# The gated convolution's three input projections as block products in seven multiplications

## The chip, the cores and the metric

One core of one Trainium2 chip runs the whole program in a single launch. The metric is the device time of that launch in microseconds (us), the median of several executions; 2549.22 us before the change (three runs, 2545.19 to 2549.35). A profile is one further execution.

## The reference

Two residual layers over 1024 tokens of width 1024, in fp32. Each layer is a mixer, a cross-attention into 256 memory tokens and a squared-ReLU MLP, each behind an RMS norm. The mixer of layer 0 is differential attention beside causal pooling; that of layer 1 is the one that is changed here:

```python
def odd_mixer(h, w_in, conv_w, w_out):
    S = h.shape[1]
    proj = h @ w_in
    b_gate = proj[..., :CONV_DIM]
    c_gate = proj[..., CONV_DIM:2 * CONV_DIM]
    z = c_gate * proj[..., 2 * CONV_DIM:]
    zp = jnp.pad(z, ((0, 0), (CONV_WIDTH - 1, 0), (0, 0)))
    y = zp[:, 0:S] * conv_w[0]
    for tap in range(1, CONV_WIDTH):
        y = y + zp[:, tap:tap + S] * conv_w[tap]
    return (b_gate * y) @ w_out
```

`h` is the normed residual stream, `w_in` is 1024 x 3072 and `w_out` 1024 x 1024.

## The kernel before

The residual stream is kept transposed: eight tiles of 128 channels by 1024 tokens. TensorE multiplies in a reduced fp32 format, so every operand is cut into a high and a low half: ScalarE copies the high half (line 72 of the profile), VectorE subtracts it from the source (line 73), and a product is the sum of three multiplications, high by high, high by low and low by high. The names `wh` and `wl` are the two halves of a weight tile; `wr` is the tile as it came from DRAM.

Two kinds of product stand in the program. `gemm` computes one tile of 128 output channels: eight tiles of input channels, three multiplications, two halves of 512 tokens, so 48 matmuls of 128 x 512, two PSUM banks. `split_gemm` computes two output tiles at once by a block scheme (2 x 2 blocks: halves of the tokens against the two tiles) in seven multiplications instead of eight: seven steps of 12 matmuls, 84 for two tiles instead of 96. For it the weights' pair is combined into four groups (`w_cut`, lines 149 to 153: four half-size VectorE operations, then a cut for each group), the input channels come as four combinations of pairs of tiles (class `Split`: `combine`, lines 259 to 262, and a cut for each), and every step's bank is added to the two output tiles by an `evac` function, since one step serves several results. Steps 0, 2, 4 and 6 write on in the same bank, so the next of them waits until the one before was read.

The MLPs (`mlp`: `m0a`, `m0b` in layer 0, `m1a`, `m1b` in layer 1) and the query projections (`c0q`, `c1q`) use `split_gemm`. The convolution (`conv_mixer`, names `cv0c` to `cv7b`) uses `gemm`: for each of eight channel tiles the products c, x and b, then on VectorE the gate, the scaling by the norm, two taps and the multiplication with b, and a cut into `Y`, the operand of the output product `cvo` (`residual`).

The convolution's operand is made at the end of the MLP before it. `m0b` runs over four chunks of the hidden width and four pairs of output tiles; in the last chunk each finished pair is scaled by the norm's weight and cut, in the product that follows. The scaling by the norm's 1 / rms comes later: squares are summed over the tiles (`m0b_acc`), TensorE transposes the sums (`m0b_n`, line 332), VectorE reduces them (333, 335), POOL takes the power (336), TensorE spreads the result (`m0b_b`, 345) and ScalarE writes it out (`m0b_rbc`).

Weights are loaded on SP's queue in the order of the list `order`, at most four tiles ahead (`WR`), each as soon as the tile whose buffer it takes has been cut; `wh` and `wl` have two buffers each, so a cut waits until TensorE is through with the group before last. Activations live in 44 equal slots. Results go to DRAM on ScalarE's queue and come back on SP's. Each engine works through its queue in order; a scheduler sets these orders by the order of the code and by priorities.

Of the kernel before, what the change touches and what calls it, by code (L numbers as in the profile page):

```python
# [40 lines left out]
def hybrid_trunk(ctx: ExitStack, tc: tile.TileContext, xT, memT, vecs, lams, rel, onehot, negrow, invcnt,  # L41
# [40 lines left out]
    order = [(FLAT, w_in[8])]  # L82
# [35 lines left out]
    def w_cut():  # L118
        u, g = state["unit"], state["group"]
        if u >= len(order):  # L120
            return
        shape = list(order[u][0])
# [7 lines left out]
        else:  # L130
            a, b = raw[0], raw[1]
            if g == 0 and u in tails:
                t = sb.tile(shape, F32, tag="wt", bufs=1, name=f"wt{u}")
# [694 lines left out]
    def residual(act, g_col, name, split=False):  # L828
# [3 lines left out]
        r = [None, None]  # L832
        for n in range(KT):
# [22 lines left out]
            else:  # L856
                ps = gemm(act, f"{name}_{n}")
# [160 lines left out]
    def mlp(l, X, nrm, g_next, name):  # L1018
# [76 lines left out]
        nx, nn = Act(), Norm(f"{name}b")  # L1095
        fin = g_next is None
        for c in range(4):
            for p in range(KT // 2):
                t, ahead = ahead, []
                tail = fin and c == 3 and p == KT // 2 - 1  # L1100
# [13 lines left out]
                todo = [rest, {1: [look]}]  # L1114
# [14 lines left out]
                def done(i, t=t, p=p):  # L1129
                    def run():  # L1130
                        n = 2 * p + i
                        if fin:
                            hd[n] = t[i]
                        else:
                            operand(nx, n, t[i], g_next, f"{name}b")
                        nn.add(t[i])
                    return run
# [140 lines left out]
```

## Time and profile before

| | us |
|---|---|
| median of three runs | 2549.22 |
| the profiled execution | 2544.53 |
| its span | 2542.8 |
| projections of the convolution, 1332.74 to 1595.67 of the span | 262.93 |
| one of their 24 products | 10.88 |
| output product `cvo` | 81.60 |

In the profile's rows PE is TensorE's matmul and PEld its weight load, DVE is VectorE, ACT ScalarE, POOL GpSimd, SP the queue that loads; L with a number is a line of the kernel. Matmul ends are modelled and matmuls overlap, so the time of many is read from the chain of waits or from a stretch, not from one duration. Idle time in a row is that of the engine just before, with what ended it.

### The profile page before, as it was taken

The page shows a single profiled execution, that of the slowest core. Times are in us where ns is not written, and L with a number is a line of the kernel's source. Part 1 is how long each engine was busy: PE and PEld are TensorE (multiplying, and loading weights), DVE is VectorE, ACT ScalarE, POOL GpSimd, SP SyncE. Part 2 cuts the span into 40 slices and gives each one's busy share as a digit, 9 for nine tenths or more (in the row PEclk, how much of TensorE's full clock was granted, in tenths as well). Part 3 has the DMA queues.
Part 4 walks back from the last instruction along what each step waited for, and adds up shares of the span by engine and source line. Part 5 has one row for each costly group of instructions (what it writes and reads, how often), then busy time and mean ns, then how long its engine had stood idle before and what let it go on. Part 6 is the DMA issues. An engine that isn't in the chain of part 4 may idle for free.

```text
span 2542.8 us, 29713 instructions
## 1 busy us (share of the span) xinstructions
PE 2498.8 (98%) x11522; PEld 2048.1 (81%) x11522; DVE 1763.8 (69%) x2339; ACT 1073.4 (42%) x1513; POOL 25.7 (1%) x24
## 2 busy tenths in 40 slices
PE   9999999999999999999999999999999999999997
PEld 6777778888878888788888888888887888778886
DVE  7777764766677777888784433576667777888876
ACT  5455664445443334443341111344544333434432
POOL 0000000000000000000000000000000000000001
PEclk9999999999999999999999999999999999999998
DMA  5111255221424346877641111422133444777752
GB/s 175 34 34 42 75 169 204 100 83 42 141 88 171 139 145 239 293 270 261 243 154 59 50 50 46 145 75 92 58 117 116 159 160 153 269 266 259 281 207 92
DMA packets 108429, 365.88 MB, mean 144 GB/s; under 512 B 12416, under 2 KB 14848, under 8 KB 108288
## 3 DMA queue, kind: packets, MB, share of 16 engines
q1 hardware_dynamic: 74880, 252.82, 29.5%
q10 hardware_dynamic: 33408, 111.16, 11.4%
q8 instruction: 91, 1.49, 0.2%
q14 instruction: 50, 0.41, 0.0%
HBM read 249.91 MB, written 114.03 MB: 143 GB/s over the span
## 4 chain that ended last, share of the span: by engine, by line
PE 89%; DVE 6%; ACT 2%; DMA 2%; issue 1%; POOL 0%; SPq 0%; ACTq 0%; DVEq 0%; POOLq 0%
PE m0a_x L277 7%; PE m1a_x L277 7%; PE m1b_x L277 7%; PE m0b_x L277 6%; PE m1a_yz L277 5%; PE m0a_yz L277 5%; PE m1b_yz L277 5%; PE m0b_yz L277 4%; PE cvo L201 3%; PE X L201 3%; PE c1o L201 3%; PE c0o L201 3%; PE kv_ps L742 3%; PE qkv L201 2%; PE c1q_x L277 2%; PE c0q_x L277 2%
## 5 line engine op out<-in xcount | busy, mean ns | idle before, releaser
L72 ACT ACTIVATE wh<-wr 128x1024 fp32r<-128x1024 f32 (+1 forms) x318 | 305.6, 961 | 777.7 <-PE m1b_yz L277 137.5
L73 DVE TENSOR_TENSOR wl<-wr,wh 128x1024 fp32r<-128x1024 f32 (+1 forms) x318 | 350.3, 1101 | 135.1 <-ACT wh L72 130.3
L72 ACT ACTIVATE wh<-wt 128x1024 fp32r<-128x1024 f32 x72 | 76.0, 1055 | 60.0 <-PE m0b_x L277 16.5
L73 DVE TENSOR_TENSOR wl<-wt,wh 128x1024 fp32r<-128x1024 f32 x72 | 87.8, 1219 | 0.9 <-ACT wh L72 0.9
L201 PE MATMUL X<-Y,wh 128*128 128x512 f32 x256 | 69.8, 389 | 0.0
L581 ACT ACTIVATE s_p<-s,s_negm 128x128 f32<-128x128 f32 (+7 forms) x64 | 47.3, 739 | 33.6 <-DVE s_negm L580 30.3
L201 PEld LDWEIGHTS X<-Y,wh 128*128 128x128 f32 x256 | 48.1, 188 | 10.0
L149 DVE TENSOR_TENSOR wt<-wr 128x512 f32<-128x512 f32 x71 | 48.8, 687 | 6.8 <-DMA wr<-in_w_dram 3.1
L150 DVE TENSOR_TENSOR wt<-wr,wt 128x512 f32<-128x512 f32 x71 | 48.9, 689 | 1.3
L152 DVE TENSOR_TENSOR wr<-wr,wr 128x512 f32<-128x512 f32 x71 | 48.7, 687 | 1.0
L153 DVE TENSOR_TENSOR wr<-wr,wt 128x512 f32<-128x512 f32 x71 | 48.6, 684 | 0.0
L1028 ACT ACTIVATE m0a_r<-m0a_r 128x1024 f32<-128x1024 f32 x32 | 33.9, 1061 | 32.0 <-DVE m0a_r L1027 31.9
L1028 ACT ACTIVATE m1a_r<-m1a_r 128x1024 f32<-128x1024 f32 x32 | 33.9, 1060 | 32.0 <-DVE m1a_r L1027 31.8
L580 DVE TENSOR_REDUCE s_negm<-s 128x1 f32<-128x128 f32 (+7 forms) x64 | 46.6, 750 | 0.2
L1042 DVE TENSOR_TENSOR m0a_r<-m0a_r,m0a_yz 128x512 f32<-128x512 f32 x32 | 21.9, 685 | 31.3 <-PE m0a_yz L277 31.1
L1042 DVE TENSOR_TENSOR m1a_r<-m1a_r,m1a_yz 128x512 f32<-128x512 f32 x32 | 21.9, 685 | 31.3 <-PE m1a_yz L277 31.1
L1038 ACT ACTIVATE m0a_r<-m0a_x 128x512 f32<-128x512 f32 x32 | 19.1, 598 | 55.7 <-PE m0a_x L277 53.8
L1038 ACT ACTIVATE m1a_r<-m1a_x 128x512 f32<-128x512 f32 x32 | 19.1, 598 | 55.5 <-PE m1a_x L277 53.9
L201 PE MATMUL X<-Y,wl 128*128 128x512 f32 x128 | 40.7, 389 | 0.0
L277 PE MATMUL m0b_x<-m0A,wh 128*128 128x512 f32 x128 | 39.5, 390 | 0.7 <-DVE m0b0h L1112 0.7
L277 PE MATMUL m0a_x<-c0o_x,wh 128*128 128x512 f32 x128 | 39.6, 390 | 0.0
L277 PE MATMUL m1a_x<-c1o_x,wh 128*128 128x512 f32 x128 | 39.5, 390 | 0.0
(2681 smaller groups left out, 7678.9 us busy)
## 6 DMA issues: line engine op xcount, KB each, us to landing
wr<-in_w_dram SPq DMA_DIRECT2D x128, 512.0 KB, 4.0
m0f<-m0a_d SPq DMA_DIRECT2D x48, 512.0 KB, 6.4
m1f<-m1a_d SPq DMA_DIRECT2D x48, 512.0 KB, 6.0
wr<-in_wkv_dram SPq DMA_DIRECT2D x32, 512.0 KB, 3.5
m0a_d<-m0a_r ACTq DMA_DIRECT2D x32, 512.0 KB, 2.8
m1a_d<-m1a_r ACTq DMA_DIRECT2D x32, 512.0 KB, 2.9
wr<-in_conv_in_dram SPq DMA_DIRECT2D x24, 512.0 KB, 3.6
wr<-in_wq_dram SPq DMA_DIRECT2D x16, 512.0 KB, 3.6
```

The source lines that it names most:

```text
L72: nc.scalar.activation(hi, src, AF.Copy)
L73: nc.vector.tensor_sub(lo, src, f32(hi))
L149: nc.vector.tensor_add(t[:, 4:], b[:, :4], b[:, 4:])
L150: nc.vector.tensor_sub(t[:, :4], a[:, :4], t[:, 4:])
L152: nc.vector.tensor_sub(a[:, :4], b[:, :4], a[:, :4])
L153: nc.vector.tensor_add(a[:, 4:], a[:, 4:], t[:, :4])
L201: nc.tensor.matmul(ps, wt[:, k, :], act.part(k, i, h), start=(k == 0 and wt is hi and i == 0), stop=(k == ks - 1 and wt is lo))
L277: nc.tensor.matmul(banks[b], w[a][:, 4 * (i % 2) + j, :], act.part(g, s, j, c), start=(new and j == 0 and n == 0), stop=(j == nk - 1 and n ...
L580: nc.vector.tensor_reduce(s["negm"][:, m : m + 1], ps[:, :L], axis=AX.X, op=ALU.max, negate=True)
L581: nc.scalar.activation(s["pr"][m][:, :L], ps[:, :L], AF.Exp, bias=s["negm"][:, m : m + 1], accum_out=s["den"][:, m : m + 1])
L742: nc.tensor.matmul(ps[mt], mem["x"][i][k // 4][:, k % 4, mt * P : (mt + 1) * P], w[j][:, kk, :], start=(k == 0 and n == 0), stop=(k == KT ...
L1028: nc.scalar.activation(t, t, AF.Square)
```

## The change

The three projections become twelve products by `split_gemm`, each for two channel tiles (`cv0c`, `cv0x`, `cv0b` to `cv3b`), 84 matmuls each. Their weights are loaded as pairs, with the input halves in the order that the block scheme wants. Their results are added up in slots of SBUF, from where VectorE makes the gate (now with the square of the norm's scale, `cv_rsq`), the taps and the closing multiplication, hung as hooks on the steps of later products.

The operand is made as a `Split`. For the pairs 0 and 1 of the MLP's last chunk combination 0 is cut at once and combinations 1 to 3 are written to DRAM and read back when they are needed; those of the pairs 2 and 3 stay in slots. The first two products, c and x of the pair 0, run in turns: two steps of the one, two of the other, by combinations 0, 1 and then 2 and 3 (`in_turns`, and the table `seq` that sets the order of the weight cuts); their hooks read, cut and add up squares. The MLP's last product takes the step order `TAIL`, and in its last chunk the inputs for the additions are asked for at step 5 instead of 1. The output product's first two tiles are begun together, six of the eight input tiles first (`late`).

```diff
--- before.py
+++ after.py
...
+            turns.add(len(order))
+            for j in range(KT // 2):
+                order += [(FLAT, conv_in[i * KT + 2 * j], conv_in[i * KT + 2 * j + 1]) for i in (1, 2, 0)]
...
+        tails.add(len(order) - 1)
...
+    seq, u = [], 0
+    while u < len(order):
+        groups = 4 if len(order[u]) > 2 else 1
+        if u in turns:
+            seq += [(u, 0), (u + 1, 0), (u, 1), (u + 1, 1), (u, 2), (u, 3), (u + 1, 2), (u + 1, 3)]
+            u += 2
+        else:
+            seq += [(u, g) for g in range(groups)]
+            u += 1
...
+                t = slot(f"wt{u}", F32, shape) if u - 1 in turns else sb.tile(shape, F32, tag="wt", bufs=1, name=f"wt{u}")
...
+    def in_turns(one, two):
+
+        for it, n in ((one, 2), (two, 2), (one, 2), (two, 2), (one, 4), (two, 4)):
+            for _ in range(n):
+                next(it, None)
...
+        two = []
+        if late:
+            two = [(w_next(), psg(f"{name}_0")), (cuts[state["used"]], psg(f"{name}_1"))]
+            state["used"] += 1
+            for ks in (range(KT - 2), range(KT - 2, KT)):
+                for w, ps in two:
+                    for k in ks:
+                        steps([(h, ps[:, half(h)]) for h in range(2)], w, act, k)
...
+                ps = two.pop(0)[1] if two else gemm(act, f"{name}_{n}")
...
+        nx, nn = Split(f"{name}x"), Norm(f"{name}b")
         fin = g_next is None
+        xd, raws_x, kept = {}, {}, {}
+
+
+        def scale(t, p, h):
+            raws_x[p, 2 * h] = slot(f"{name}x{p}_r{h}")
+            for i in range(2):
+                nc.scalar.activation(raws_x[p, 2 * h][:, i * H : (i + 1) * H], t[i][:, half(h)], AF.Copy,
+                                     scale=col(g_next + 2 * p + i))
+
+        def sums(p):
+            raws_x[p, 1], raws_x[p, 3] = (slot(f"{name}x{p}_t{i}") for i in range(2))
+            raws_x[p, 3] = raws_x[p, 3][:, :H]
+            combine(raws_x[p, 0], raws_x[p, 2], raws_x[p, 1], raws_x[p, 3])
+
+        def first_group(p):
+            nx.group(0, p, raws_x[p, 0])
+
+        def put(p):
+            for g in range(1, 4):
+                xd[p, g] = dp.tile([P, S if g < 3 else H], F32, name=f"{name}x{p}_d{g}")
+                nc.scalar.dma_start(xd[p, g], raws_x.pop((p, g)))
+
+        def get(g):
+            for p in range(2):
+                x = slot(f"{name}xf{g}_{p}")
+                raws_x[p, g] = x if g < 3 else x[:, :H]
+                nc.sync.dma_start(raws_x[p, g], xd[p, g])
+
+        def made(g, *ps):
+            for p in ps:
+                nx.group(g, p, raws_x.pop((p, g)))
...
-                todo = [rest, {1: [look]}]
+                todo = [rest, {5 if c == 3 and not fin else 1: [look]}]
...
+                if tail and not fin:
+                    todo.append({2: [lambda: get(1)], 4: [lambda: made(1, 0)],
+                                 5: [lambda: scale(t, p, 0), lambda: first_group(p), lambda: made(1, 1)],
+                                 6: [lambda: made(1, 2), lambda: get(2)]})
...
+                elif p < 2:
+                    rest = {1: [lambda t=t, p=p: scale(t, p, 0), lambda t=t, p=p: scale(t, p, 1)],
+                            2: [lambda p=p: first_group(p), lambda p=p: sums(p)], 3: [lambda t=t: nn.add(t[0])],
+                            4: [lambda p=p: put(p), lambda t=t: nn.add(t[1]), keep]}
+                elif p == 2:
+                    rest = {2: [lambda t=t, p=p: scale(t, p, 0), lambda t=t, p=p: scale(t, p, 1)],
+                            3: [lambda p=p: first_group(p), lambda p=p: sums(p)], 4: [keep]}
+                    kept[2] = t
+                else:
+                    scale(t, p, 1)
+                    sums(p)
+                    made(1, 3)
+                    nx.late = ({2: [lambda: get(3)], 3: [lambda: made(2, 0)], 4: [lambda: made(2, 3)],
+                                5: [lambda: made(3, 0, 1)], 6: [lambda: made(3, 2, 3)]},
+                               {2: [lambda: made(2, 1)], 3: [lambda: made(2, 2)],
+                                4: [lambda: nn.add(kept[2][0]), lambda: nn.add(kept[2][1]), keep],
+                                5: [lambda t=t: nn.add(t[0])], 6: [lambda t=t: nn.add(t[1]), nn.stage1]})
...
-        hooks = with_norm(nrm)
-        Y = Halves()
-        for j in range(KT):
-            nm = f"{name}{j}"
-            psc = gemm(X, f"{nm}c", hooks.pop(0) if hooks else None)
-            cg, z = slot(f"{nm}_cg"), slot(f"{nm}_z")
-            if nrm.rbc is not None:
-                nc.vector.tensor_mul(cg, psc, nrm.rbc)
-            psx = gemm(X, f"{nm}x", hooks.pop(0) if hooks else None)
+        Y, ys = Halves(), {}
+        sq = {}
+
+        def product(nm, hooks, first=False, run=True):
+            r = [slot(f"{nm}_r{n}") for n in range(2)]
+
+            def evac(n, h, ps, new):
+                d = r[n][:, half(h)]
+                if new:
+                    nc.scalar.activation(d, ps, AF.Copy)
+                else:
+                    nc.vector.tensor_add(d, d, ps)
+
+            steps = split_steps(X, nm, evac, hooks, first=first)
+            if not run:
+                return r, steps
+            for _ in steps:
+                pass
+            return r
+
+        def parts(k):
+            return lambda: Y.put(f"{name}g{k}_", k, ys.pop(k))
+
+        def squared():
+            sq[0] = slot(f"{name}_rsq")
+            nc.scalar.activation(sq[0], nrm.rbc, AF.Square)
+
+        for j in range(KT // 2):
+            nm, last = f"{name}{j}", j == KT // 2 - 1
             if j == 0:
-                nc.vector.tensor_mul(cg, psc, nrm.rbc)
-            nc.vector.tensor_mul(z, psx, nrm.rbc)
-            nc.vector.tensor_mul(z, z, cg)
-            y = slot(f"{nm}_y")
-            nc.scalar.activation(y, z, AF.Copy, scale=col(C_CONV + 16 + j))
-            nc.vector.scalar_tensor_tensor(y[:, 1:], z[:, : S - 1], col(C_CONV + 8 + j), y[:, 1:],
-                                           op0=ALU.mult, op1=ALU.add)
-            nc.vector.scalar_tensor_tensor(y[:, 2:], z[:, : S - 2], col(C_CONV + j), y[:, 2:],
-                                           op0=ALU.mult, op1=ALU.add)
-            nc.vector.tensor_mul(y, y, nrm.rbc)
-            psb_ = gemm(X, f"{nm}b")
-            nc.vector.tensor_mul(y, y, psb_)
-            Y.put(f"{nm}g", j, y)
-        return residual(Y, g_next, f"{name}o", split=True)
+                c, one = product(f"{nm}c", X.late[0], first=True, run=False)
+                x, two = product(f"{nm}x", X.late[1], run=False)
+                in_turns(one, two)
+            else:
+                c = product(f"{nm}c", merged(before, {4: [parts(0)]} if last else {}))
+                x = product(f"{nm}x", {1: [parts(1)], 3: [parts(2)]} if last else {})
+
+            def gate(n, c=c, x=x):
+                def run():
+                    nc.vector.tensor_mul(c[n], c[n], x[n])
+                    nc.vector.tensor_mul(c[n], c[n], sq[0])
+                return run
+
+            def taps(n, z=c, j=j):
+                def run():
+                    k = 2 * j + n
+                    y = ys[k] = slot(f"{name}_y{k}")
+                    nc.scalar.activation(y, z[n], AF.Copy, scale=col(C_CONV + 16 + k))
+                    for d in (1, 2):
+                        nc.vector.scalar_tensor_tensor(y[:, d:], z[n][:, : S - d], col(C_CONV + 8 * (2 - d) + k),
+                                                       y[:, d:], op0=ALU.mult, op1=ALU.add)
+                return run
+
+            def scaled(n, j=j):
+                return lambda: nc.vector.tensor_mul(ys[2 * j + n], ys[2 * j + n], nrm.rbc)
+
+            hooks = {0: [gate(0)], 1: [taps(0)], 2: [gate(1)], 3: [taps(1)], 4: [scaled(0)], 5: [scaled(1)]}
+            if j == 0:
+                hooks = {1: [nrm.stage2, squared], 2: [gate(0)], 3: [taps(0)], 4: [gate(1)], 5: [taps(1)],
+                         6: [scaled(0), scaled(1)]}
+            if last:
+                hooks = merged(hooks, {3: [parts(3)], 5: [parts(4)], 6: [parts(5)]})
+            b = product(f"{nm}b", hooks)
+
+            def times(n, j=j, b=b):
+                return lambda: nc.vector.tensor_mul(ys[2 * j + n], ys[2 * j + n], b[n])
+
+            before = {1: [times(0)], 2: [times(1)]}
+        for n in range(2):
+            times(n)()
+            parts(KT - 2 + n)()
+        return residual(Y, g_next, f"{name}o", split=True, late=True)
...
+    g["conv_in"] = tiles(a["conv_w_in"][0])[..., halves, :]
```

The rows that follow are the engines' instruction streams as built. In the names, `m0b3h6` and `m0b3h7` are the MLP's last two output tiles, `m0x_g_p` with h or l is the half of combination g of pair p, `m0xf` a combination read back from DRAM, `wl98`, `wl99` and `wl100` are the low halves of the convolution's first weights for c, x and b; L1112 became L1170 and L333, L335 became L352, L354.

VectorE at the end of the MLP, before:

```order
L1112 TENSOR_TENSOR m0b3h7_10594<-m0b3h7_10594,m0b3_3_yz_10707 128x512
L73 TENSOR_TENSOR wl97_3_10783<-wr97_1_10512,wh97_3_10782 128x512
L1112 TENSOR_TENSOR m0b3h7_10594<-m0b3h7_10594,m0b3_3_x_10706 128x512
L1112 TENSOR_TENSOR m0b3h6_10592<-m0b3h6_10592,m0b3_3_yz_10707 128x512
L73 TENSOR_TENSOR wl98_0_10821<-wr98_0_10650,wh98_0_10820 128x1024
L76 SCALAR_TENSOR_TENSOR m0b_x6l_10840<-m0b3h6_10592,vec_76,m0b_x6h_10839 128x1024
L1112 TENSOR_TENSOR m0b3h7_10594<-m0b3h7_10594,m0b3_3_x_10706 128x512
L324 TENSOR_TENSOR m0b_acc_10450<-m0b_acc_10450,m0b_sq_10843 128x1024
L76 SCALAR_TENSOR_TENSOR m0b_x7l_10847<-m0b3h7_10594,vec_76,m0b_x7h_10846 128x1024
L324 TENSOR_TENSOR m0b_acc_10450<-m0b_acc_10450,m0b_sq_10850 128x1024
L73 TENSOR_TENSOR wl99_0_10858<-wr99_0_10652,wh99_0_10857 128x1024
```

The same place now:

```order
L1170 TENSOR_TENSOR m0b3h7_10697<-m0b3h7_10697,m0b3_3_x_10734 128x512 x2
L73 TENSOR_TENSOR m0x_0_3l_10850<-m0x3_r0_10846,m0x_0_3h_10849 128x1024
L1170 TENSOR_TENSOR m0b3h7_10697<-m0b3h7_10697,m0b3_3_yz_10735 128x512
L1170 TENSOR_TENSOR m0b3h6_10695<-m0b3h6_10695,m0b3_3_yz_10735 128x512
L73 TENSOR_TENSOR m0x_1_1l_10854<-m0xf1_1_10778,m0x_1_1h_10853 128x1024
L1170 TENSOR_TENSOR m0b3h6_10695<-m0b3h6_10695,m0b3_3_x_10734 128x512
L73 TENSOR_TENSOR wl98_0_10872<-wr98_0_10665,wh98_0_10871 128x1024
L73 TENSOR_TENSOR m0x_1_2l_10881<-m0x2_t0_10797,m0x_1_2h_10880 128x1024
L162 TENSOR_TENSOR wr98_0_10665<-wr98_1_10667,wr98_0_10665 128x512
L163 TENSOR_TENSOR wr98_0_10665<-wr98_0_10665,wt98_10873 128x512
L267 TENSOR_TENSOR m0x3_t0_10904<-m0x3_r1_10901,m0x3_r0_10846 128x512
L73 TENSOR_TENSOR wl99_0_10921<-wr99_0_10820,wh99_0_10920 128x1024
```

The cut of `wl98` stood ahead of the last addition to `m0b3h7`; it now stands behind the last addition to `m0b3h6` and behind the cut of `m0x_1_1l`, whose source comes from DRAM.

TensorE at the start of the convolution now:

```order
L295 MATMUL m0b3_3_x_10734<-m0A3_2_3h_10338,wl97_3_10817 128x512
L295 MATMUL cv0c_x_10918<-m0x_0_0h_10469,wh98_0_10871 128x512
L295 MATMUL cv0c_x_10918<-m0x_0_0l_10470,wh98_0_10871 128x512
L295 MATMUL cv0c_yz_10919<-m0x_0_0h_10469,wh98_0_10871 128x512
L295 MATMUL cv0c_yz_10919<-m0x_0_0l_10470,wh98_0_10871 128x512
L295 MATMUL cv0c_x_10918<-m0x_0_0h_10469,wl98_0_10872 128x512
L295 MATMUL cv0c_x_10918<-m0x_0_1h_10622,wh98_0_10871 128x512
```

Four matmuls with `wh98` stand ahead of the first that needs `wl98`; before, the first product's matmuls had the same high and low weights in turn.

VectorE where the norm's sums are reduced, before:

```order
L324 TENSOR_TENSOR m0b_acc_10450<-m0b_acc_10450,m0b_sq_10850 128x1024
L73 TENSOR_TENSOR wl99_0_10858<-wr99_0_10652,wh99_0_10857 128x1024
L333 TENSOR_REDUCE m0b_ms_8465<-m0b_n0_10894 128x4
L333 TENSOR_REDUCE m0b_ms_8465<-m0b_n1_10900 128x4
L335 TENSOR_SCALAR m0b_ms_8465<-m0b_ms_8465 128x8
L73 TENSOR_TENSOR wl100_0_10929<-wr100_0_10786,wh100_0_10928 128x1024
```

And now, at the end of the x product:

```order
L343 TENSOR_TENSOR m0b_acc_10492<-m0b_acc_10492,m0b_sq_11186 128x1024
L1240 TENSOR_TENSOR cv0x_r0_10916<-cv0x_r0_10916,cv0x_yz_10956 128x512
L160 TENSOR_TENSOR wt100_11179<-wr100_0_11067,wt100_11179 128x512
L73 TENSOR_TENSOR wl100_0_11178<-wr100_0_11067,wh100_0_11177 128x1024
L352 TENSOR_REDUCE m0b_ms_8465<-m0b_n0_11189 128x4
L162 TENSOR_TENSOR wr100_0_11067<-wr100_1_11069,wr100_0_11067 128x512
L163 TENSOR_TENSOR wr100_0_11067<-wr100_0_11067,wt100_11179 128x512
L352 TENSOR_REDUCE m0b_ms_8465<-m0b_n1_11195 128x4
L73 TENSOR_TENSOR wl100_1_11221<-wt100_11179,wh100_1_11220 128x1024
L354 TENSOR_SCALAR m0b_ms_8465<-m0b_ms_8465 128x8
```

The two reductions and the scalar step stood together; now two combinations and a cut of the b weights stand among them, and the reduction follows the cut of `wl100_0`.

More of the change, by code (lines that the diff above doesn't have):

```diff
@@ L81, in hybrid_trunk @@
     FLAT = (P, KT, P)
-    order = [(FLAT, w_in[8])]
+    order, tails, turns = [(FLAT, w_in[8])], set(), set()
     for h in range(1, 4):
@@ L98, in hybrid_trunk @@
         order += [(FLAT, w2[l, c, 2 * p], w2[l, c, 2 * p + 1]) for c in range(4) for p in range(KT // 2)]
-    tails = {len(order) - 1}
+        tails.add(len(order) - 1)
     raws, cuts = {}, []
-    state = dict(loaded=0, held=0, group=0, unit=0, used=0)
+    state = dict(loaded=0, held=0, cut=0, used=0)
+    seq, u = [], 0
[7 more added lines that the diff above has]
+            u += 1
     def w_load():
@@ L118, in w_cut @@
     def w_cut():
-        u, g = state["unit"], state["group"]
-        if u >= len(order):
+        if state["cut"] >= len(seq):
             return
+        u, g = seq[state["cut"]]
         shape = list(order[u][0])
@@ L161, in w_cut @@
         cuts.append((hi, lo))
-        state["group"] += 1
+        state["cut"] += 1
         if done:
             state["held"] -= min(len(raw), 2)
-            state["unit"] += 1
-            state["group"] = 0
             w_load()
     def w_next():
-        while len(cuts) < state["used"] + 2 and state["unit"] < len(order):
+        while len(cuts) < state["used"] + 2 and state["cut"] < len(seq):
             w_cut()
@@ L264, in split_gemm, with split_steps @@
     def split_gemm(act, name, evac, hooks=None, first=False, tail=False):
+        for _ in split_steps(act, name, evac, hooks, first, tail):
+            pass
[3 more added lines that the diff above has]
+                next(it, None)
+    def split_steps(act, name, evac, hooks=None, first=False, tail=False):
         x, yz = psb(f"{name}_x", tag="f"), psg(f"{name}_yz")
@@ L1099, in mlp @@
                 t, ahead = ahead, []
-                tail = fin and c == 3 and p == KT // 2 - 1
+                tail = c == 3 and p == KT // 2 - 1
                 def look():
@@ L1127, in keep, with done @@
                         h_store(2 * p + i, t[i], f"{name}b{c}")
[L1129 to L1137, printed above, removed]
                 if c < 3:
                     rest = {2: [keep]}
-                elif tail:
-                    hd.update({2 * p + i: t[i] for i in range(2)})
-                    squares_of(0, 1)()
+                elif fin:
+                    def done(i, t=t, p=p):
+                        def run():
+                            hd[2 * p + i] = t[i]
+                            nn.add(t[i])
+                        return run
+                    rest = {1: [done(0)], 2: [done(1)]}
+                    if tail:
+                        hd.update({2 * p + i: t[i] for i in range(2)})
+                        squares_of(0, 1)()
+                        rest = {}
+                elif p < 2:
[15 more added lines that the diff above has]
+                                5: [lambda t=t: nn.add(t[0])], 6: [lambda t=t: nn.add(t[1]), nn.stage1]})
@@ L1144, in mlp @@
                     rest = {}
-                else:
-                    rest = {1: [done(0)], 2: [done(1)], 4: [] if fin else [keep]}
         for fns in merged(rest).values():
```

16 lines of the change are left out of this document (7 added, 9 removed).

## The prediction

> **What bounds the kernel now.** I read the page's span and busy shares first, then the chain of waits.
>
> ```profile
> span 2542.8 us, 29713 instructions
> PE 2498.8 (98%) x11522; PEld 2048.1 (81%) x11522; DVE 1763.8 (69%) x2339; ACT 1073.4 (42%) x1513; POOL 25.7 (1%) x24
> PE 89%; DVE 6%; ACT 2%; DMA 2%; issue 1%; POOL 0%; SPq 0%; ACTq 0%; DVEq 0%; POOLq 0%
> ```
>
> TensorE is busy for 98% of the span and is 89% of the chain: time goes away only with matmuls, or with the few gaps. Next, the stretch that is changed: the chain in order of time (start, length, work), and busy time by stage (length, then PE, PEld, DVE, ACT, POOL, clock, DMA share, GB/s).
>
> ```profile
> 1330.02 2.72 PE m0b_x L277 x12
> 1332.74 6.80 PE cv0c L201 x30
> 1339.54 0.87 PE m0b_n L332 x8
> ...
> 1345.87 0.87 PE m0b_b L345 x8
> ...
> 1356.31 10.88 PE cv0b L201 x48
> ...
> 1584.79 10.88 PE cv7b L201 x48
> 1595.67 81.60 PE cvo L201 x360
> ```
>
> ```profile
> 1022.00:1332.40 310.40, 307.13 (x1347) 251.93 (x1346) 253.74 (x316) 127.08 (x139) 0.00 (x0) 1.00 0.68 241
> 1332.40:1595.30 262.90, 262.90 (x1170) 217.96 (x1169) 109.85 (x101) 46.34 (x51) 1.64 (x1) 1.00 0.19 59
> 1683.70:1800.00 116.30, 113.44 (x596) 96.16 (x594) 77.84 (x119) 59.34 (x113) 1.64 (x1) 1.00 0.24 82
> ```
>
> The three projections run from 1332.74 to 1595.67: 262.93 us = 24 products of 10.88 and two pieces of 0.87 for the norm. No gap is in it. A matmul is 10.88 / 48 = 0.227 us; in the MLP, where the seven-multiplication form is already used, twelve take 2.72 us: 0.227 too. So the form itself costs nothing per matmul. VectorE is busy for 109.85 of 262.90 us here, ScalarE for 46.34.
>
> **What is removed.** 24 products of 48 matmuls (1152) become 12 of 7 x 12 = 84 (1008). 144 x 0.2267 = **32.6 us** off the path. The norm's two pieces stay. Everything below is what may be given back.
>
> **VectorE's added work.** These rows give durations and pitch (start to start, when nothing is waited for):
>
> ```profile
> 1315.42 0.69 DVE L153 TENSOR_TENSOR wr<-wr,wt 128x512 f32<-128x512 f32 x1
> 1316.02 1.22 DVE L73 TENSOR_TENSOR wl<-wt,wh 128x1024 fp32r<-128x1024 f32 x1
> 1317.16 0.68 DVE L1112 TENSOR_TENSOR m0b3h<-m0b3h,m0b_x 128x512 f32<-128x512 f32 x1
> 1330.06 0.69 DVE L1112 TENSOR_TENSOR m0b3h<-m0b3h,m0b_yz 128x512 f32<-128x512 f32 x1 [2.03 <-PE m0b_yz L277]
> 1330.92 1.23 DVE L73 TENSOR_TENSOR wl<-wr,wh 128x1024 fp32r<-128x1024 f32 x1 [0.18 <-ACT wh L72]
> 1332.07 1.28 DVE L76 SCALAR_TENSOR_TENSOR m0b_x6l<-m0b3h,vec,m0b_x6h 128x1024 fp32r<-128x1024 f32 x1
> 1333.26 0.68 DVE L1112 TENSOR_TENSOR m0b3h<-m0b3h,m0b_x 128x512 f32<-128x512 f32 x1
> ```
>
> 512 columns step by 0.60 us (1315.42 to 1316.02), 1024 by 1.14 (1316.02 to 1317.16), the scaled form by 1.19 (1332.07 to 1333.26). One new product: 3.5 weight cuts, 4 weight combinations, 3 additions of results = 3 x 1.14 + 8 x 0.60 = 8.2 us in the 84 x 0.2267 = 19.04 us that TensorE takes. A pair of channel tiles adds 4 gate multiplies, 4 scaled taps and 4 more multiplies: 8 x 1.14 + 4 x 1.19 = 13.9. So 3 x 8.2 + 13.9 = 38.6 of 57.1 us, 68%; in the last pair 12 half cuts of the gated result come on top, 45.8, 80%. But most of it falls into the third product of a pair: 8.2 + 4 x 1.14 + 4 x 1.19 + 2 x 1.14 = 19.8 us in 19.04, and 23.4 in the last. The two closing multiplies come one product later, where there is room. In queue order the cut of the next weights stands ahead of them, so I take 0 for it, and price the other end as a rival. ScalarE has 3.5 cuts and 4 copies of 0.6 us per product, some 6.1 of 19.04: hidden.
>
> **The turn into the convolution** is where a wait appears. By VectorE's rows shown with the change, the cut of the first weights (`wl98`) stood ahead of the MLP's last addition; now it stands behind that and behind the cut of an operand read back from DRAM (`m0x_1_1l`). Count from the MLP's last matmul (0 = 1332.74). Step five of seven ends at -5.44; its two additions begin there; ScalarE scales and cuts what they give, by these rows (mean ns):
>
> ```profile
> L842 ACT ACTIVATE cvo_r<-cvoh,vec 128x512 f32<-128x512 f32 x16 | 10.8, 716 | 8.5 <-DVE cvoh L858 6.3 <-DVE cvoh L849 2.2
> L72 ACT ACTIVATE wh<-wt 128x1024 fp32r<-128x1024 f32 x16 | 17.0, 1062 | 19.2 <-PE m0b_x L277 16.5 <-DVE wl L73 2.7
> ```
>
> That is -4.8, -4.1, -3.0. Then VectorE: cut to -1.9, two additions to -0.7, the second operand cut to 0.5 (its high half is done at -0.6, behind `wh98`, whose buffer comes free at -2.72), the last addition to 1.15, `wl98` to 2.4. TensorE has four matmuls that need only the high half (0.9 us), then waits: **1.5 us** lost. Bounds: 0.5 if two additions slip forward, 3 if ScalarE is one cut late.
>
> After that both products take turns, which gives each combination 10.9 us (two products of 24 matmuls) before it is needed. VectorE's queue then holds 9 items to the next weights (`wl99`, 6.4 against 6.9 when TensorE gets there), and stays ahead: combination 1 is complete at 10.4 against 12.3, combination 2 at 25.6 against 26.4, combination 3 at 28.6 against 30.7. 0 taken; the margins are 0.5 to 2 us.
>
> **The norm's second piece.** TensorE transposes the sums (`m0b_n`) in the last step of x, VectorE reduces them, POOL takes the power, TensorE needs it 15 matmuls into the b product. Before:
>
> ```profile
> 1340.02 1.29 DVE L333 TENSOR_REDUCE m0b_ms<-m0b_n 128x4 f32<-128x512 f32 x2 [1.30 <-PE m0b_n L332]
> 1341.34 0.17 DVE L335 TENSOR_SCALAR m0b_ms<-m0b_ms 128x8 f32<-128x8 f32 x1
> 1341.59 1.64 POOL L336 TENSOR_TENSOR m0b_rcol<-m0b_ms,mhalf 128x8 f32<-128x8 f32 x1 [611.00 <-DVE m0b_ms L335]
> ```
>
> By the rows shown with the change, the reductions now follow a weight cut, and two weight combinations and another cut stand among them and the scalar step. With the 1.5 us, x's last step begins at 36.8 (thirteen steps of 2.72). From the addition there: 37.5, 38.1, 39.2, 39.9, 41.1, 41.7, 42.9, 43.0, and POOL's 1.64 to 44.8. TensorE arrives at 36.8 + 0.9 + 0.87 + 1.8 + 3.4 = 43.8: **1.0 us** lost (0 to 2.5).
>
> **The rest.** The first two output products begin in turns: the second's high weights wait for a buffer that the last conv matmul frees, 1.06 us against four matmuls, 0.9: 0.2 us. The tail order of the MLP's last product only permutes seven steps: 0. The operand's trip through DRAM and the later request for the inputs of the MLP's last products:
>
> ```profile
> m0f<-m0a_d SPq DMA_DIRECT2D x48, 512.0 KB, 6.4
> m0b3h<-m0b2hd SPq DMA_DIRECT2D x8, 512.0 KB, 6.1
> wr<-in_conv_in_dram SPq DMA_DIRECT2D x24, 512.0 KB, 3.6
> ```
>
> ```profile
> 1194.92 8.90 DMA m0f<-m0a_d
> ```
>
> The inputs are asked for some 9 us ahead (6.1 needed, 8.9 at worst): 0. Combination 1 of the first two pairs is asked for before the last product begins, -19; at 8.9 us it is there by -10, needed at -1.6. On SP's queue combinations 2 and 3 stand behind the second half of the x weights (its buffer is free at about -6): there by 4, needed at 15. The b weights behind them wait for a buffer until 24.5, so the reads cost them nothing. Cover 9 to 11 us: 0 taken.
>
> **Sum.** 32.6 - 1.5 - 1.0 - 0.2 = 29.9 us. The profiled execution took 2544.53 us around its span of 2542.8; it becomes 2514.6. The three timed runs have their median 4.7 above it: 2549.22 becomes 2519.3. I take 2518, with 2512 (all hidden, from the profiled time) to 2522 for this case.
>
> **Rivals.**
> *VectorE binds in the third products.* For: 19.8 and 23.4 us of work in 19.04. Against: 68% over a pair, and the late work isn't needed until the next product. If TensorE pays each surplus: 3 x 0.8 + 4.4 = 6.8 more lost, 2549.2 - 23.1 = 2526.
> *The read-back is late at the turn.* `wl98` stands behind `m0x_1_1l`, so each us that this read lands after -1.6 is one of TensorE's. For: reads of 8.9 us exist. Against: 9 us of cover. With 5 us late: 2524.
> The Trainium skill ("TensorE: Matmul & The Clock Gate", Part 1) says that a gap above about 3.4 us halves the clock for as long, an estimated 1.7 us more in this rival. The longest wait that this trace shows near here is the one below, with the clock at 1.00 in that stretch, so it does not test the rule.
>
> ```profile
> PE c1q_x L277 <- ACT c1q_r L920: 1.0, 1, 1.0
> ```
>
> *Weights bind: slower.* A step lasts 2.72 us instead of a whole product's 10.88, and the two weight buffers turn every 5.44: release, 1.06 on ScalarE, VectorE's queue, 1.22. If that were late by 32.6 / 48 = 0.68 us in each of the 48 groups, the gain is gone; at 0.9 the time is 2560. For: VectorE's items are long, and a cut can stand behind two or three. Against: the MLP stage lives with this form, at VectorE 253.74 of 310.40 us, and TensorE's idle there is 3.3 us in 64 groups, 0.05 each:
>
> ```profile
> PE m0b_x L277 <- DVE wl L73: 0.4, 1, 0.4
> ```
>
> **How the numbers follow.** Forecast 0.80; VectorE binds 0.10; read-back late 0.05; slower 0.03; no difference 0.02 (the last rival with 0.6 to 0.75 us a group). Under 0.2% a measurement can't tell from no change. Faster 0.95, same 0.02, slower 0.03. The range takes the forecast and the first two rivals: 2511 to 2530.
>
> **What would show it.** TensorE's matmuls fall by 144; the projections take some 233 us between the MLP and the output product instead of 262.93; a TensorE wait of about 1.5 us on VectorE's `wl` right at the turn, one of about 1 us on POOL at `m0b_b`, none above 0.5 us in the products 1 to 3. Waits on `wl` in every third product would show the first rival, a wait of `m0x` on a DMA the second. I am wrong if TensorE's idle time in the stretch exceeds 5 us.

## The result and the profile after

The changed kernel takes 2522.01 us (median of 4 runs, 2519.47 to 2526.86) beside 2547.2 us before (4 runs, 2544.54 to 2549.35): 0.9904 of the time, with a 95% interval of 0.9885 to 0.9923. That is faster, by 25 us where 31 were forecast, and within the range of 2511 to 2530. Runs of one kernel lie up to 7 us apart, so what single microseconds are worth is read below in the traces, as the *stretch*: from the convolution's first matmul to the output product's first. It was 262.93 us (1332.58 to 1595.51) and is 238.21 (1333.61 to 1571.82).

The page of the change: span, busy time by engine, and the engines' shares of the chain.

```profile
span 2520.0 us, 29709 instructions
PE 2469.5 (98%) x11378; PEld 2020.2 (80%) x11378; DVE 1843.9 (73%) x2465; ACT 1134.2 (45%) x1610; POOL 28.4 (1%) x24
PE 88%; DVE 6%; ACT 3%; issue 1%; DMA 1%; POOL 0%; SPq 0%; DVEq 0%; ACTq 0%; POOLq 0%
```

TensorE has 144 matmuls less (11522 to 11378), as announced. By stage (length, then PE, PEld, DVE, ACT, POOL, clock, DMA share, GB/s) the stretch, which had no gap before, has some now:

```profile
1333.50:1571.70 238.20, 232.98 (x1026) 191.55 (x1025) 179.99 (x209) 100.07 (x134) 4.28 (x1) 0.99 0.19 59
```

238.20 less 232.98 is 5.2 us in which TensorE stands still, and the clock's mean is 0.99, not 1.00. TensorE's waits from 1200 to 1700 us (total, times, longest) name the two places:

```profile
PE m0b_b L364 <- POOL m0b_rcol L355: 3.6, 1, 3.6
PE cv0c_x L295 <- DVE wl L73: 1.6, 1, 1.6
...
```

The chain in order of time (start, length, work) shows both:

```profile
1335.09 1.15 DVE wl L73
...
1336.28 1.88 PE cv0c_x L295 x7
...
1377.67 4.29 POOL m0b_rcol L355
...
1382.01 1.52 PE m0b_b L364 x8
1383.52 3.23 PE cv0b_yz L295 x9
1386.76 2.74 PE cv0b_x L295 x12
```

The turn waits for the first weights, as forecast. At the norm's second piece POOL's power takes 4.29 us; before the same instruction on the same 128x8 values took 1.64. And behind the wait the eight transposes take 1.52 us instead of 0.87, the next nine matmuls 3.23 instead of 9 x 0.2267 = 2.04: 1.8 us more. The books of the stretch: 1008 x 0.2267 + 1.74 = 230.2 without any wait, + 1.6 + 3.6 + 1.8 = 237.2. Of the last 1.0 us, 0.3 is the restart at the turn (seven matmuls in 1.88 instead of 1.59). Another 0.3 is how the two waits are counted: from the modelled end of the matmul ahead, 0.39 us after its start, and not from its step of 0.227. The rest lies in pieces of 0.05 to 0.15: two short halts of TensorE, at 1359 and 1360 us, and one in each later b product.

Why was POOL slow? VectorE and POOL at that moment (start, length, engine, line, operation, operands):

```profile
1377.43 0.16 DVE L354 TENSOR_SCALAR m0b_ms<-m0b_ms 128x8 f32<-128x8 f32 x1
1377.51 2.35 DVE L1268 TENSOR_TENSOR cv0c_r<-cv0c_r,cv0x_r 128x1024 f32<-128x1024 f32 x2
1379.78 0.68 DVE L159 TENSOR_TENSOR wt<-wr 128x512 f32<-128x512 f32 x1
1380.49 0.69 DVE L160 TENSOR_TENSOR wt<-wr,wt 128x512 f32<-128x512 f32 x1
1377.67 4.28 POOL L355 TENSOR_TENSOR m0b_rcol<-m0b_ms,mhalf 128x8 f32<-128x8 f32 x1 [646.36 <-DVE m0b_ms L354]
```

Before, POOL worked from 1341.59, and VectorE, through with its scalar step at 1341.51, came next to this:

```profile
1345.24 1.22 DVE L73 TENSOR_TENSOR wl<-wr,wh 128x1024 fp32r<-128x1024 f32 x1 [3.72 <-ACT wh L72]
```

So VectorE was idle while POOL worked. Now two gate multiplications (c by x) and a weight combination, all with both inputs in SBUF, run back to back until 1380.4. The power ends at 1381.95; take off its usual 1.64 and it began its work at about 1380.3, just when VectorE's row of such operations has its first gap: the combination of 1379.78 is through at 1380.4, by the usual step of 0.60, and the next begins at 1380.49. The trace of before already held one such case, in the kernel's attention: a power beside a weight cut with both inputs in SBUF.

```profile
278.75 1.21 DVE L73 TENSOR_TENSOR wl<-wr,wh 128x1024 fp32r<-128x1024 f32 x1
278.91 2.54 POOL L336 TENSOR_TENSOR sub_rcol<-sub_ms,mhalf 128x8 f32<-128x8 f32 x1 [71.04 <-DVE sub_ms L335]
```

2.54 is 1.64 and the 0.9 or so that the cut still had to run. **Theory:** a VectorE operation with two inputs in SBUF keeps POOL from starting; POOL comes in at VectorE's next gap. **Rivals:** POOL is slow there for a reason of its own (it had been idle for 646 us), or any work of VectorE slows it. For the slow matmuls, the theory is the clock after a gap; the rival is the transposes themselves.

### The profile page after: what moved, and what is told of

Same layout as the page of the kernel before. It is cut to its first block, busy times and chain, and to the rows that moved or that the text cites. A ratio compares the mean times of both kernels' runs of the same rounds, so it can differ in the third digit from the quotient of the medians.

```text
span 2520.0 us, 29709 instructions
## 1 busy us (share of the span) xinstructions
PE 2469.5 (98%) x11378; PEld 2020.2 (80%) x11378; DVE 1843.9 (73%) x2465; ACT 1134.2 (45%) x1610; POOL 28.4 (1%) x24
## 4 chain that ended last, share of the span: by engine, by line
PE 88%; DVE 6%; ACT 3%; issue 1%; DMA 1%; POOL 0%; SPq 0%; DVEq 0%; ACTq 0%; POOLq 0%
PE m0a_x L295 7%; PE m1a_x L295 7%; PE m1b_x L295 7%; PE m0b_x L295 6%; PE m0a_yz L295 5%; PE m1a_yz L295 5%; PE m1b_yz L295 5%; PE m0b_yz L295 4%; PE cvo L209 3%; PE X L209 3%; PE c0o L209 3%; PE c1o L209 3%; PE kv_ps L761 3%; PE qkv L209 2%; PE c1q_x L295 2%; PE c0q_x L295 2%
## 5 line engine op out<-in xcount | busy, mean ns | idle before, releaser
L72 ACT ACTIVATE wh<-wr 128x1024 fp32r<-128x1024 f32 (+1 forms) x330 | 313.1, 949 | 644.7 <-PE m1b_yz L295 132.5
L73 DVE TENSOR_TENSOR wl<-wr,wh 128x1024 fp32r<-128x1024 f32 (+1 forms) x330 | 358.4, 1086 | 156.3 <-ACT wh L72 151.7
L72 ACT ACTIVATE wh<-wt 128x1024 fp32r<-128x1024 f32 x84 | 88.6, 1055 | 83.5 <-PE m1b_x L295 16.1
L73 DVE TENSOR_TENSOR wl<-wt,wh 128x1024 fp32r<-128x1024 f32 x84 | 102.3, 1218 | 1.4 <-ACT wh L72 1.4
L209 PE MATMUL cvo<-cvg,wh 128*128 128x512 f32 x256 | 69.8, 389 | 0.0
L159 DVE TENSOR_TENSOR wt<-wr 128x512 f32<-128x512 f32 x82 | 56.3, 686 | 6.5 <-DMA wr<-in_w_dram 3.0
L160 DVE TENSOR_TENSOR wt<-wr,wt 128x512 f32<-128x512 f32 x82 | 56.4, 688 | 1.6
L162 DVE TENSOR_TENSOR wr<-wr,wr 128x512 f32<-128x512 f32 x82 | 56.3, 687 | 1.1
L209 PEld LDWEIGHTS cvo<-cvg,wh 128*128 128x128 f32 x256 | 48.0, 188 | 10.4 <-ACT wh L72 0.4
L209 PE MATMUL cvo<-cvg,wl 128*128 128x512 f32 x128 | 40.6, 389 | 0.0
```

Of the source, the lines that this page charges most:

```text
L72: nc.scalar.activation(hi, src, AF.Copy)
L73: nc.vector.tensor_sub(lo, src, f32(hi))
L159: nc.vector.tensor_add(t[:, 4:], b[:, :4], b[:, 4:])
L160: nc.vector.tensor_sub(t[:, :4], a[:, :4], t[:, 4:])
L162: nc.vector.tensor_sub(a[:, :4], b[:, :4], a[:, :4])
L209: nc.tensor.matmul(ps, wt[:, k, :], act.part(k, i, h), start=(k == 0 and wt is hi and i == 0), stop=(k == ks - 1 and wt is lo))
```

## The experiments

Each of them but the fifth is a single execution, so what it shows is read from its trace.

### The gate behind the power

```diff
-def gate(n, c=c, x=x):
+def gate(n, c=c, x=x, j=j):
...
-nc.vector.tensor_mul(c[n], c[n], x[n])
-nc.vector.tensor_mul(c[n], c[n], sq[0])
+p, q = (c[n], x[n]) if j else (x[n], sq[0])
+nc.vector.tensor_mul(p, p, q)
+nc.vector.tensor_mul(c[n], c[n], sq[0] if j else x[n])
```

> In the first pair the gate multiplies x by the squared norm first and c by x second, so that VectorE can't start the gate before POOL's power is done. Theory (VectorE's operations with both inputs in SBUF keep POOL from starting): only two weight combinations of 0.60 us still stand beside the power, it takes 2.2 to 2.8 us instead of 4.28, TensorE's wait at m0b_b falls from 3.6 to 1.5 to 2.1 us, and as the gap is then short the matmuls behind it step at 0.227 us again (m0b_b x8 0.87 instead of 1.52): some 3.4 us less between the MLP and the output product. Rival (POOL is slow there for a reason of its own, such as its long idle time before): the power stays at 4.3 and the wait at 3.6.

VectorE and POOL in order of time, and then the chain behind the power:

```profile
1380.69 0.17 DVE L354 TENSOR_SCALAR m0b_ms<-m0b_ms 128x8 f32<-128x8 f32 x1
1380.81 0.69 DVE L159 TENSOR_TENSOR wt<-wr 128x512 f32<-128x512 f32 x1
1381.54 0.69 DVE L160 TENSOR_TENSOR wt<-wr,wt 128x512 f32<-128x512 f32 x1
1380.94 2.06 POOL L355 TENSOR_TENSOR m0b_rcol<-m0b_ms,mhalf 128x8 f32<-128x8 f32 x1 [645.78 <-DVE m0b_ms L354]
```

```profile
1383.05 1.09 PE m0b_b L364 x8
1384.14 2.08 PE cv0b_yz L295 x9
```

The power takes 2.06 us: 1.64 and 0.42, about what was left of the one combination that ran when POOL was released. It got in at the gap before the second, so the time lies below my 2.2 to 2.8, which had counted both. POOL had been idle as long as ever (645.78 us), so the first rival falls. The operation that held it here is an addition of 512 columns, not a multiplication. TensorE's wait is 1.4 us, the nine matmuls take 2.08 again, the stretch is 234.43: 3.8 us less, of which 2.2 is the wait and 1.6 the matmuls.

### The same load beside two other powers

```diff
 nc.gpsimd.tensor_tensor(self.rcol[:, cs], self.ms[:, cs], mhalf[:, cs], op=ALU.pow)
+if self.name == "c0o":
+    for _ in range(2):
+        nc.vector.tensor_mul(acc, acc, acc)
+if self.name == "c1o":
+    for _ in range(4):
+        nc.vector.tensor_add(acc[:, :H], acc[:, :H], ps.rearrange("p a b -> p (a b)"))
```

> Extra work for VectorE beside two other powers of POOL that take 1.64 us with VectorE idle: at c0o a multiplication of 1024 columns with both inputs in SBUF (1.14 us) right behind the step that releases POOL, at c1o two additions of 512 columns with one input in PSUM (1.2 us). Theory (the inputs in SBUF count): c0o_rcol 2.5 to 2.8 us, c1o_rcol stays at 1.64; TensorE's wait at c0o_b grows from 0.2 to about 1.2. Rival (any work of VectorE slows POOL): both about 2.6. Rival (VectorE does nothing to POOL): both 1.64.

```profile
733.62 1.22 DVE L358 TENSOR_TENSOR c0o_acc<-c0o_acc 128x1024 f32<-128x1024 f32 x1
733.75 2.59 POOL L355 TENSOR_TENSOR c0o_rcol<-c0o_ms,mhalf 128x8 f32<-128x8 f32 x1 [220.22 <-DVE c0o_ms L354]
...
1905.25 1.41 DVE L361 TENSOR_TENSOR c1o_acc<-c1o_acc,c1o_n 128x512 f32<-128x512 f32 x2
1905.47 1.64 POOL L355 TENSOR_TENSOR c1o_rcol<-c1o_ms,mhalf 128x8 f32<-128x8 f32 x1 [219.69 <-DVE c1o_ms L354]
```

The code adds two multiplications at `c0o` and four additions at `c1o`; the rows show those that ran beside the power. One multiplication from SBUF makes the power 2.59 us instead of 1.64. Two additions that take one input from PSUM cover most of the other power, and it stays at 1.64. So VectorE's being busy isn't what matters; where its inputs lie is. Nor is it addition against multiplication: the combination that held POOL in the first experiment was an addition too, with both inputs in SBUF. TensorE's wait at `c0o_b` came to 2.2 us, not 1.2: one of the two multiplications had been put ahead of the step that releases POOL.

### The norm's second piece two steps later

```diff
-hooks = {1: [nrm.stage2, squared], 2: [gate(0)], 3: [taps(0)], 4: [gate(1)], 5: [taps(1)],
+hooks = {3: [nrm.stage2, squared, gate(0)], 4: [taps(0), gate(1)], 5: [taps(1)],
          6: [scaled(0), scaled(1)]}
```

> The norm's second piece and the square behind it go from step 1 of the first b product to step 3, the gate and the taps after it; TensorE comes to m0b_b some 4.8 us later. The power stays slow, since the gate's first multiplications still stand beside it (about 4.3 us), but nobody waits for it: TensorE's wait of 3.6 us goes to 0 to 0.2. If the slow matmuls behind the wait come from the gap (clock), they go as well and the gain is 3.6 + 1.8 = 5.4 us, stretch 232.8 instead of 238.2; if the slow matmuls come from the transposes themselves, m0b_b x8 stays at 1.5 us and the gain is 3.6. If VectorE is short of time later in this product, a wait on wl of 0.5 us or more appears before the next product.

The power still takes 4.28 us. TensorE's waits from 1200 to 1700 us:

```profile
PE cv0c_x L295 <- DVE wl L73: 1.6, 1, 1.6
...
PE cv1c_x L295 <- DVE wl L73: 0.2, 1, 0.2
```

The wait of 3.6 is gone and 0.2 is new, at the next product's weights. The stretch is 233.26 us: 4.95 less, more than the wait alone is worth. So the slow matmuls belonged to the gap: with the gap they go. The same eight transposes are there, without a wait ahead of them, and the matmul behind them starts 0.79 us after the first (1382.02 to 1382.81).

### The first weights ahead of the read-back operand

```diff
 todo.append({2: [lambda: get(1)], 4: [lambda: made(1, 0)],
-             5: [lambda: scale(t, p, 0), lambda: first_group(p), lambda: made(1, 1)],
+             5: [lambda: scale(t, p, 0), lambda: first_group(p)],
...
-nx.late = ({2: [lambda: get(3)], ...
+nx.late = ({0: [lambda: made(1, 1)], 2: [lambda: get(3)], ...
```

> The cut of the second operand that is read back for combination 1 goes from step five of the MLP's last product to the start of the convolution's first, so that on VectorE the cut of the first weights stands ahead of it. Theory (the 1.6 us at the turn are VectorE's queue: one cut of 1.14 us too many ahead of the weights): the wait on wl falls from 1.6 to 0 to 0.4 us. Price: combination 1 is then complete only about when it is needed, a wait of 0 to 0.5 us some 11 us later. Rival (the weights' high half or ScalarE sets it): the wait stays above 1.2.

```profile
PE m0b_b L364 <- POOL m0b_rcol L355: 3.6, 1, 3.6
PE cv0c_x L295 <- DVE m0x_1l L73: 0.2, 1, 0.2
```

The wait of 1.6 us on the weights is gone, and the operand that was put back is 0.2 late: the stretch is 237.11, 1.1 less. But the edit moved more than the cut. On VectorE the last addition of the MLP (0.60 us) now stands behind the cut of the weights too, which starts 0.32 us ahead of the convolution's first matmul (1331.83 against 1332.15) where in the change it started 1.41 behind it (1335.02 against 1333.61). So the 1.6 us were VectorE's queue, as the theory said, but not the one cut of 1.14 us alone: cut and addition together are 1.74.

### Both moves, beside the change itself

> The two moves together: the norm's second piece in step 3 of the first b product, and the first weights' cut ahead of the read-back operand's. The moves alone took the stretch from the MLP to the output product from 238.2 to 233.3 and 237.1 us. If they lie apart, they add up: 232.2 us, 6.0 less than the change (2516 where the change takes 2522); if the first only hands its wait on to the next product (VectorE late with the weights after the gate), a new wait of over 1 us appears and less than 5 is left.

> The change itself once more, on the same chip as the two moves together: 2522 us as before, waits of 1.6 and 3.6 us, POOL's power 4.3 us. If the power's length were chance, it would differ here.

Beside before on the same chip (2545.39 us) the change took 2522.22 us, 0.9904 (0.9889 to 0.9919), with its power at 4.28 us and the waits of 3.6 and 1.6 once more, stretch 238.24. Both moves took 2517.96 us (2514.62 to 2520.39), 0.9889 (0.9873 to 0.9906). The two intervals overlap, but all four of its times lie below the change's four (2521.76 to 2522.52). What each move is worth is read from the traces. All that is left of TensorE's waits from 1200 to 1600 us, and then the stretch as a stage:

```profile
PE cv0c_x L295 <- DVE m0x_1l L73: 0.2, 1, 0.2
PE cv1c_x L295 <- DVE wl L73: 0.2, 1, 0.2
```

```profile
1332.70:1564.80 232.10, 231.67 (x1026) 190.12 (x1025) 179.94 (x209) 100.09 (x134) 4.28 (x1) 1.00 0.19 60
```

232.15 us, 6.1 less than the change: the two add up (4.95 + 1.1). The profiled executions took 2515.64 and 2521.76 us: 6.1 again. This version is ahead of before by 30.8 us in the stretch.

### No turns in the first pair

```diff
-turns.add(len(order))
...
-c, one = product(f"{nm}c", X.late[0], first=True, run=False)
-x, two = product(f"{nm}x", X.late[1], run=False)
-in_turns(one, two)
+c = product(f"{nm}c", X.late[0], first=True)
+x = product(f"{nm}x", X.late[1])
...
-nx.late = ({2: [lambda: get(3)], 3: [lambda: made(2, 0)], 4: [lambda: made(2, 3)],
+nx.late = ({2: [lambda: get(3), lambda: made(2, 0)], 3: [lambda: made(2, 1), lambda: made(2, 2)], 4: [lambda: made(2, 3)],
...
-{2: [lambda: made(2, 1)], 3: [lambda: made(2, 2)],
- 4: [lambda: nn.add(kept[2][0]), ...
+{4: [lambda: nn.add(kept[2][0]), ...
```

> The first pair's two products one after the other, not in turns; what makes the combinations is put ahead of their use. By VectorE's queue, counted as in the prediction, combination 1 comes at about the 42nd matmul of c (no wait or 0.5 us), combination 2 some 1 to 2 us late, combination 3 about 1 us late, the x weights 0.5 to 1: TensorE waits 2 to 4 us more on VectorE within the first two products, stretch 240 to 242 instead of 238.2. Rival (the turns hide nothing, the combinations come in time anyway): within 0.5 us of 238.2. Rival (each combination is needed before VectorE can be there): over 6 us more.

```profile
PE m0b_b L363 <- POOL m0b_rcol L354: 4.1, 1, 4.1
PE cv0c_x L294 <- ACT cv0c_r L1236: 2.4, 1, 2.4
PE cv0c_x L294 <- DVE wl L73: 1.6, 1, 1.6
```

The stretch is 241.72, 3.5 us more: the turns are worth that. Of it 2.4 is the new wait and 0.5 the longer wait at the power, which itself still takes 4.28 us. The size was right, the place was not. The wait of 2.4 us is on ScalarE, where the cuts of a weight group and of an operand (1340.44 and 1341.40) stand ahead of the copy of a result (1342.35); VectorE, which I had counted, was in time.

### More work for VectorE in the third products

```diff
+def more(n, x=x):
+    def run():
+        for _ in range(2):
+            nc.vector.tensor_mul(x[n], x[n], x[n])
+    return run
...
+hooks = merged(hooks, {2: [more(0)], 4: [more(1)]})
```

> Four more multiplications of 1024 columns (both inputs in SBUF) in each third product of a pair, 4.6 us of VectorE's time, on the x that is used up. VectorE's work in such a product goes from 19.8 to 24.4 us where TensorE takes 19.04, over a pair from 38.6 to 43.2 of 57.1. My theory (late work carries over into the next products): TensorE loses 0 to 2 us a pair, stretch 239 to 246, part of it one more us at m0b_b where a multiplication stands beside POOL's power (4.3 becomes 4.9 to 5.5). Rival (VectorE binds in the product itself): 4 to 5 us a pair, stretch 255 or more, waits on wl in each.

TensorE's waits from 1320 to 1640 us, and then three pieces of time behind the wait at `cv2c`, which ends at 1464.02 (the clock is the third number from the end):

```profile
PE m0b_b L364 <- POOL m0b_rcol L355: 4.1, 1, 4.1
PE cv2c_x L295 <- DVE wl L73: 3.2, 1, 3.2
PE cv3c_x L295 <- DVE wl L73: 3.2, 1, 3.2
PE cv0c_x L295 <- DVE wl L73: 1.6, 1, 1.6
PE cv1c_x L295 <- DVE wl L73: 1.5, 1, 1.5
PE cvo L209 <- ACT wh L72: 1.4, 2, 0.9
PE cvo L209 <- DVE wl L73: 1.1, 1, 1.1
PE cv3b_x L295 <- DVE wl L73: 0.8, 1, 0.8
```

```profile
1464.00:1465.00 1.00, 0.98 (x4) 0.85 (x5) 1.00 (x2) 0.34 (x1) 0.00 (x0) 1.00 0.00 0
1465.00:1468.00 3.00, 3.00 (x8) 2.35 (x8) 3.00 (x5) 0.85 (x2) 0.00 (x0) 0.50 0.00 0
1469.00:1472.00 3.00, 3.00 (x15) 2.46 (x14) 1.43 (x3) 1.06 (x1) 0.00 (x0) 1.00 0.00 0
```

The stretch is 250.26 us, 12 more: above my 239 to 246 and below the rival's 255. In pairs two and three 3.2 of the 4.56 us come back as a wait for the next pair's weights, and each such wait costs some 1.7 us of slow matmuls besides. So VectorE carries over only about 4.56 - 3.2 = 1.4 us from such a third product: the cut of the next weights (from 1462.75) stands in its queue behind the last of the extra work (from 1461.01). After the first pair 1.5 us come back. The last three rows lie where the output product begins: there the last pair's extra work costs 3.3 us of waits, most of them behind the stretch.

## Why the prediction was right, and where it was off

- **The 32.6 us.** Right. 144 matmuls went, at 0.227 us each. With the two waits taken away the stretch is 30.8 us shorter than before; 0.4 of the remaining 1.8 is waits, the rest is in small pieces.
- **The turn, 1.5 us.** Right, 1.6, by the mechanism given: VectorE's queue, in which the cut of an operand and the last addition stood ahead of the weights; the fourth experiment moved both.
- **The turns' margins, 0.** Right for the change: no wait above 0.15 us between the turn and the norm. What they hide, by the sixth experiment, is ScalarE's queue, with cuts ahead of the copy of a result; ScalarE I had called hidden from its share alone.
- **The norm's second piece, 1.0 us (0 to 2.5): this step failed.** The time at which POOL is released was well counted: x's last step plus the queue of VectorE. Mis-sized was "POOL's 1.64 to 44.8". I took the one row in which VectorE was idle and didn't ask what VectorE would be doing at that moment after the change; a row of 2.54 us stood in the same trace. The wait was 3.6 us, above my upper bound, and 1.8 us of slow matmuls came with it: 5.4 for a term of 1.0. The Trainium skill ("SBUF — State Buffer", Who interferes with whom) says that a VectorE instruction with two inputs in SBUF contends with a GpSimd instruction that reads SBUF, and that one with at most one such input, outside the 2-port modes, does not. The traces agree on both: 2.06, 2.59 and 4.28 us against 1.64.
- **The output product, 0.2 us.** Right, about 0.3, by the mechanism given. In the chain its first four matmuls start at 1571.98 and take 0.91 us, and the other 356 start at 1572.91 and take 80.99: 81.92 in all, where it took 81.60 before. The load of the second tile's high weights onto TensorE waited 0.44 us, until 1572.91, for ScalarE's cut, which the last conv matmul had released.
- **VectorE binds (0.10).** Did not happen: no wait in the products 1 to 3. But the room was 1.4 us in a third product, far less than "68% over a pair" made it look.
- **The read-back (0.05) and the weights (0.03).** Did not happen: no wait on a DMA in the stretch, and behind the turn no group of the products waited for its weights. Of the six reads the four of 512 KB took 6.1 us in the median and the slowest of all 7.6.
- **The sum.** Against the profiled execution 29.9 us were forecast and 22.7 came (2544.53 to 2521.83). Of the difference of 7.2, 2.6 is the wait at the norm above what I gave it, 1.8 the slow matmuls, 0.1 the turn, some 0.9 the small pieces. Another 1.0 us was lost ahead of the stretch. It is there already at the program's first power (`n_rcol`, at 32.98 us before and 33.98 now), and over the traced executions this point lies anywhere from 32.98 to 33.99, so it is scatter from the start of the program and not the change's. Behind the stretch 0.9 was lost; 0.3 of it is the start of the output product, and the rest I can't place.
- **The sign of being wrong.** I wrote that I would be wrong if TensorE's idle time in the stretch exceeded 5 us. It is 5.2. The forecast's sign and range held, but its account of the stretch did not. 2522.01 us stands at the very edge of the 2512 to 2522 that I gave the forecast's own case; that it lies well inside the whole range is luck, since that was widened for rivals that did not come about.

## What to carry to other kernels

The same POOL instruction took 1.64 to 4.81 us here, by what VectorE did beside it: before pricing one from a row, look at what VectorE does beside that row, and what it will do after the change. Operations with both inputs in SBUF, back to back, held POOL until the first gap. A small step on another engine that TensorE will wait for can be asked for some matmuls later at little cost (0.2 us here), if its result isn't needed at once. And a long wait can cost more than its length: those of 3.2 us and more did here, by some 1.7 us each, those of 2.4 and less did not.

## What the runs showed that I had not expected

**POOL is kept out by a row of operations, not by one.** In the change POOL was released 0.16 us after the first gate multiplication began, and did not get in between the first and the second, nor before the combination that followed at once; it began at the first gap, 2.64 us later. In the first experiment it got in after a single combination, since the second began 0.1 us after the first was through (0.60 after its start, by its step). Is that gap POOL's doing? No: the second combination reads what the first writes, and in the change's trace ten other such pairs between 1008 and 1536 us, with POOL idle, start 0.72 to 0.73 us apart as well. In the last experiment, where a third multiplication stood in the row, the power took 4.81 us: it began at 1379.9, when the third was through.

**The clock behind a wait.** The granted clock in the change, behind the wait of 3.6 us (from 1378.4 to 1382.0):

```profile
1382.00:1384.00 2.00, 1.99 (x10) 1.90 (x11) 0.00 (x0) 1.04 (x2) 0.00 (x0) 0.63 0.00 0
1384.00:1385.00 1.00, 1.00 (x3) 0.74 (x3) 0.00 (x0) 0.97 (x2) 0.00 (x0) 0.50 0.00 0
1385.50:1386.00 0.50, 0.50 (x3) 0.40 (x2) 0.00 (x0) 0.00 (x0) 0.00 (x0) 0.57 0.00 0
1386.00:1387.00 1.00, 1.00 (x6) 0.83 (x5) 0.14 (x1) 0.44 (x1) 0.00 (x0) 1.00 0.00 0
```

The mean of 0.63 over the first two us says that it falls from 1.00 to 0.50 some 0.5 us after the matmuls have begun again; it is back at about 1385.9, some 3.4 us later. The waits of 3.2 us in the last experiment did the same, and that of 4.1 us in the sixth; waits of 1.4, 1.6 and 2.4 us did not. The Trainium skill ("TensorE: Matmul & The Clock Gate", Part 1) states a free-running window of about 3.4 us: an idle one halves the clock, a busy one restores it. The trace agrees in the length of the slow piece. It does not show a window that has to be idle throughout. At `cv2c` in the last experiment the matmuls around the wait start here:

```profile
1460.40 0.39 PE L295 MATMUL cv2c_yz<-m0x_0l,wh 128*128 128x512 f32 x1
1464.02 0.50 PE L295 MATMUL cv2c_x<-m0x_0h,wl 128*128 128x512 f32 x1 [3.24 <-DVE wl L73]
```

By the usual step TensorE stood still for 3.4 us, but the clock falls only at about 1465.0, so the 3.4 us ahead of that fall hold 1 us of matmuls. How much idleness is enough is not shown; the runs say only that a wait of 3.2 us was, and one of 2.4 was not.

**A slow stretch without a wait.** In the first experiment's execution the clock was halved for 10 us in the attention stage, which no kernel here changed and where TensorE waits at most 0.9 us; in the change's own execution and in that of before it was 1.00 there, in that of the second experiment 0.66. The first experiment's rows:

```profile
299.00:309.00 10.00, 10.00 (x28) 7.27 (x28) 4.84 (x9) 2.73 (x7) 0.00 (x0) 0.50 0.19 52
309.00:319.00 10.00, 10.00 (x56) 7.71 (x55) 4.22 (x8) 7.49 (x13) 0.00 (x0) 1.00 0.31 105
```

28 matmuls instead of some 50 in 10 us: from the power ahead of this piece (at 279 us) to the one behind it that execution took 4.4 us longer than the change's, 79.2 instead of 74.8. The seven times of before in the fifth experiment lie in two groups 4 us apart (2545.06 to 2545.66, and 2549.15 and 2549.21), and those of both moves too. The mean clock on record for the two long ones is 0.996, for the five short ones 0.997 or 0.998; 10 us at 0.50 would take 0.002 off. So this is likely the same thing, but those runs left no trace, and what sets it off stays open.
